# Small matmuls of the head groups in alternating array halves, with two heads' products in two PSUM banks

## The chip, the core and the metric

The kernel runs on one core of a Trainium2 chip. The core has five engines with a queue each: TensorE (PE; its weight loads are shown apart as PEld), VectorE (DVE), ScalarE (ACT), GpSimd (POOL) and SyncE (SP, which here issues most DMAs). Each queue is worked in order, and semaphores tie the queues together. The metric is the device time of one execution in microseconds; lower is better.

## The reference, cut to what matters

The program is one inference step of one decoder layer for a prompt of 512 tokens and 8 single-token samples: modulated RMSNorm, one input projection, two head groups, an output projection and a SwiGLU FFN. The change lies in the two head groups. All data are float32.

The first group is 16 attention heads of 64 columns; for the prompt the three dilated windows fold into one score matrix with a bias per distance:

```
z[q,k]  = (Q_h[q] . K_h[k]) * rn[q] + T_h[q,k]        # q, k = 0..511, causal
out_h   = softmax(z) @ V_h
```

The second group is 16 RWKV-7 heads with a state of 64 x 64 each:

```
S_t = S_{t-1} diag(w_t) + (S_{t-1} a_t) b_t^T + v_t k_t^T ;   y_t = S_t r_t
```

## The kernel before, in words

The 512 tokens of an RWKV head are cut into 8 chunks of 64. Inside a chunk the recurrence is a triangular system, solved with matrix products; between chunks only the state is passed on. Heads are taken in pairs: head 0 of a pair lives in partitions 0 to 63 (`hb[0]`), head 1 in partitions 64 to 127 (`hb[1]`), so most matmuls of this stage use one half of the array's rows, of its columns, or one quarter. There are 8 pairs in each group.

`rwkv_pair(pr)` does for one pair, in this order:

- the Gram products `pg`: per half `i` of the sequence and head `h`, four matmuls of 64 rows x 128 columns, which VectorE masks into `GM` (L901);
- a solve of 16 x 16 blocks: `GM` is written to DRAM (`nd`, L910), read back with one block per partition (`i16`, in the trace `i<-nd`, L915), inverted by nineteen VectorE instructions (`itmp`, `xi`, L926 to L938), written out again (`xd`, L941) and read back as `XX` (four DMAs, L944);
- from the 16 x 16 inverses to the 64 x 64 one by matmuls of quarter array size: `pq` from `XX`, then `px` and `pxt`, then `pq2` and `px2` of 32 x 32 (the trace shows these two as `pq<-X2T,GM` and `px<-X,Q`);
- `pbk`, `pat`, `pgv`, `pu` and last `pxa`, which ScalarE and VectorE empty into `AR` (L1019) and `Mt` (L1020).

`chain(pr)` then passes the state through the 8 chunks (`pch`, with a ScalarE copy into `Sall` after each) and computes the outputs (`zy`, `z2`). `attn_pair(pr)` does one pair of attention heads: scores `pz`, softmax on VectorE and ScalarE, transposes `pzt`, values `po`. Between them stand matmuls of a weight stream for the modulation (`ada`), filler work with no hurry.

Two things set the order. A list puts the pieces in program order (`r0 r1 c0 a0 r2 c1 S a1 r3 c2 a2 ...`: r is `rwkv_pair`, c `chain`, a `attn_pair`, S the RWKV step of the samples), and a scheduler at build time then orders each engine's queue by what it takes to be ready. A tile of a pool can be written only when the tile that last had its buffer has been read; within a pool the buffers go round in program order. The PSUM pools of this stage:

```
NPS, NPA, NPT, NPG, SP, SPL, PER = 1, 2, 2, 1, 1, 8, 4
psa = lambda name: psB.tile([P, 512], F32, tag="psa", name=name, bufs=NPA)
pst = lambda name: psB.tile([P, 512], F32, tag="pst", name=name, bufs=NPT)
pa = lambda name: psB.tile([P, 512], F32, tag="pa", name=name, bufs=NPG)
```

Before the change `pa` (one bank) holds only Gram products. `psa` (two banks) holds everything else in `rwkv_pair`: per pair `pq`, `px`, `pxt`, `pq2`, `px2`, `pbk` twice, `pat`, `pgv`, `pu` twice, `pxa` twice. `pst` (two banks) holds the attention tiles `pz`, `pzt` and `po`. A float32 matmul is two passes through the array, so the trace has two matmul records for each one in the code.

Of the kernel before, what the change touches and what calls it, by code (L numbers as in the profile page):

```python
# [12 lines left out]
ALU = mybir.AluOpType  # L13
# [4 lines left out]
P = 128  # L18
# [60 lines left out]
def hymba_step(tc, a):  # L79
# [97 lines left out]
    with ExitStack() as top:  # L177
# [627 lines left out]
        with ExitStack() as wk_stack:  # L805
# [73 lines left out]
            def rwkv_pair(pr):  # L879
# [88 lines left out]
                for c in range(2):  # L968
                    top_, bot = slice(c * 64, c * 64 + 32), slice(c * 64 + 32, c * 64 + 64)
                    for i in range(8):  # L970
                        mm(pq2[bot, i, :32], gm(i // 2, c, i % 2, top_, slice(c * 64 + 32, c * 64 + 64)), X2T[top_, i, :32])
                Q2 = tq2(f"Q2{pr}", 256).rearrange("p (i t) -> p i t", i=8)
                px2 = psa(f"px2{pr}").rearrange("p (i t) -> p i t", i=8)
                for c in range(2):
                    top_, bot = slice(c * 64, c * 64 + 32), slice(c * 64 + 32, c * 64 + 64)
                    ac.copy(Q2[bot], pq2[bot, :, :32])
                    for i in range(8):
                        mm(px2[top_, i, :32], Q2[bot, i, :], X2[bot, i, 32:])
                    ve.tensor_copy(X2[top_, :, 32:], px2[top_, :, :32])
# [11 lines left out]
                for c in range(2):  # L991
                    for b in range(4):
# [3 lines left out]
                for c in range(2):  # L996
                    for i in range(8):
                        mm(pgv[hb[c], i * 64 : i * 64 + 64], gm(i // 2, c, i % 2, hb[1 - c], hb[c]), UV[hb[1 - c], i // 2 * 2 + c, i % 2, :])
                ac.copy(AG[:, :, 0, :], pgv.rearrange("p (i e) -> p i e", e=E))
                XA = txa(f"XA{pr}", 512).rearrange("p (b h e) -> p b h e", b=4, h=2)  # L1000
                for q in range(2):
                    pu = psa(f"pu{pr}{q}").rearrange("p (b h x e) -> p b h x e", b=2, h=2, x=2)
                    for c in range(2):
                        for i in range(4):
                            mm(pu[hb[c], i // 2, i % 2], X2[hb[c], 4 * q + i, :], AG[hb[c], 4 * q + i])
                    for c in range(2):
                        ac.copy(UV[hb[c], 4 * q + c : 4 * q + 4 : 2], pu[hb[c], :, :, 0, :])
                    ac.copy(XA[:, 2 * q : 2 * q + 2], pu[:, :, :, 1, :])
                Mt = wl.tile([P, 4, 2, E], F32, tag="mt", name=f"Mt{pr}", bufs=NMT)
                for c in range(2):  # L1010
                    pxa = psa(f"pxa{pr}{c}")
                    for i in range(8):
                        o_ = i // 2 * 64
                        mm(pxa[hb[i % 2], o_ : o_ + 64], AG[hb[c], i, 1, :], X2[hb[c], i, :])
                    for i in range(8):
                        b, h = i // 2, i % 2
                        o_ = 256 + b * 64
                        mm(pxa[hb[h], o_ : o_ + 64], XA[hb[c], b, h, :], BKt[hb[c], 2 * b + c, h * 64 : h * 64 + 64])
                    ac.copy(ARv[:, :, 3 * c, :], pxa[:, :256].rearrange("p (b t) -> p b t", b=4))  # L1019
                    ve.tensor_tensor(Mt[:, :, c, :], pxa[:, 256:].rearrange("p (b t) -> p b t", b=4),  # L1020
                                     eye2.unsqueeze(1).to_broadcast([P, 4, E]), op=ALU.add)
                return lambda: chain(pr, AR, Mt, UV, BKt, GM, gm, bv)

            def chain(pr, AR, Mt, UV, BKt, GM, gm, bv):
# [17 lines left out]
                for q in range(2):  # L1042
                    zy = psz(f"zy{pr}{q}").rearrange("p (c e) -> p c e", c=4)
                    for c in range(4):
                        if q or c:
                            mm(zy[:, c, :], AR[:, (4 * q + c) * 128 : (4 * q + c + 1) * 128], S[:, 4 * q + c, :])
                    for c in range(2):
                        n0 = 2 if q == 0 and c == 0 else 0
                        u = UV[hb[c], 4 * q + c + n0 : 4 * q + 4 : 2].rearrange("p b h e -> p b (h e)")
                        ve.tensor_add(u, u, zy[hb[c], c + n0 :: 2, :])  # L1050
                    q2 = slice(2 * q, 2 * q + 2)
                    if q == 0:
                        gp.memset(Y[64:, 0], 0.0)
# [4 lines left out]
                    for c in range(4):  # L1058
                        b, R_ = 2 * q + c // 2, hb[1 - c % 2]
                        for h in range(2):  # L1060
                            mm(z2[R_, c // 2, h * 64 : h * 64 + 64], gm(b, c % 2, h, slice(0, 128), R_), UV[:, 4 * q + c, h, :])
                    ve.tensor_add(Y[:, q2], Y[:, q2], z2[:, :2])
# [99 lines left out]
            def attn_pair(pr):  # L1162
# [14 lines left out]
                def scores(qi):  # L1177
                    nk = 128 * (qi + 1)
                    for h in range(2):
                        hr = slice(h * 64, h * 64 + 64)  # L1180
                        pz = pst(f"pz{pr}{h}{qi}")
                        mm(pz[:, :nk], q[hr, qi * 128 : (qi + 1) * 128], kn[hr, :nk])
                        z = tz(f"z{pr}{h}{qi}", nk)
                        ve.scalar_tensor_tensor(z, in0=pz[:, :nk], scalar=rn[:, qi, h : h + 1], in1=Ts[h][:, 384 - 128 * qi :],  # L1184
# [8 lines left out]
                def values(qi):  # L1193
# [9 lines left out]
                    for h in range(2):  # L1203
# [262 lines left out]
```

## Time and profile before

| what | value |
|---|---|
| median of 3 runs | 3371.26 us (3350.44 to 3377.52) |
| the profiled execution | 3378.55 us; span of its instructions 3376.8 us |
| TensorE busy, share of the span | 88% |
| VectorE busy | 73% |
| ScalarE busy | 38% |
| mean granted TensorE clock | 0.918 of full speed |
| stage of the head groups | from about 895 us to about 1505 us of the span |

The profile is a record of one execution; its times start with the span. "Busy" is the union of the instructions' durations on an engine. A matmul's record ends when its last result leaves the array, while the next one starts much earlier, so a busy TensorE need not be a TensorE at its peak: what a matmul costs in a row of equal ones is the distance from start to start.

### The profile page before, as it was taken

The numbers are of one execution on the slowest core, as the hardware profiler recorded it, in microseconds if no ns is written. First come the engines' busy times: TensorE is split into PE (matmuls) and PEld (weight loads), VectorE is DVE, ScalarE is ACT, GpSimd is POOL, SyncE is SP. The second block draws the span as 40 slices with busy tenths as digits, with TensorE's granted clock in tenths as the row PEclk, the third lists the DMA queues.
The fourth block names the chain that finished last, engine by engine and source line by source line (L and its number), as shares of the span: only waits on it lengthen the run. The fifth ranks groups of instructions, "written<-read, shape, count | busy, mean of one in ns | idle before, by whom it ended". The sixth has DMA issues, their size and how long they took to land.

```text
span 3376.8 us, 59004 instructions
## 1 busy us (share of the span) xinstructions
PE 2981.6 (88%) x23282; PEld 2629.4 (78%) x23282; DVE 2480.9 (73%) x4846; ACT 1278.0 (38%) x2041; POOL 212.9 (6%) x216
## 2 busy tenths in 40 slices
PE   6987888999889999977977999999999987888988
PEld 2477787889746666656967999999999987787878
DVE  5666788777557455656878787778777788889786
ACT  3353343334223343444434333333333343334333
POOL 0100122110012111101000000000000000000000
PEclk8978999999858798887988999999999998999999
DMA  7744444444579798933322333333333332323223
GB/s 255 232 139 154 147 159 157 133 146 140 175 223 282 201 239 232 249 103 117 109 78 69 113 104 104 108 112 107 113 101 113 109 125 96 99 94 119 85 94 104
DMA packets 449194, 476.17 MB, mean 141 GB/s; under 512 B 84110, under 2 KB 360547, under 8 KB 448916
## 3 DMA queue, kind: packets, MB, share of 16 engines
q1 hardware_dynamic: 438736, 452.16, 43.4%
q10 hardware_dynamic: 7428, 11.65, 1.0%
q0 software_dynamic: 2752, 8.60, 0.8%
q8 instruction: 182, 2.98, 0.4%
q14 instruction: 96, 0.79, 0.1%
HBM read 409.10 MB, written 68.17 MB: 141 GB/s over the span
## 4 chain that ended last, share of the span: by engine, by line
PE 35%; DVE 28%; DMA 23%; issue 5%; ACT 5%; SPq 1%; POOL 1%; ACTq 0%; DVEq 0%; POOLq 0%
PE ada L90 4%; DMA raw_ada<-in_ada_w 2%; SPq L130 1%; PE po L90 1%; DVE x_a L125 1%; PE lx L90 1%; PE pg L90 1%; PE pz L90 1%; PE px L90 1%; DMA K<-in_cache_k 1%; PE pch L90 1%; PE pq L90 1%; DMA xb<-in_ada_w 1%; PE q22M L90 1%; PE q31M L90 1%
## 5 line engine op out<-in xcount | busy, mean ns | idle before, releaser
L90 PE MATMUL ada<-raw_ada,c_st 128*32 128x512 f32 x584 | 123.7, 763 | 17.5 <-DMA raw_ada<-in_ada_w 16.8
L90 PE MATMUL ada<-xb,c_st 128*32 128x512 f32 x184 | 69.9, 673 | 15.9 <-DMA xb<-in_ada_w 13.8
L1037 ACT ACTIVATE Sall<-pch,ppl 64x64 f32<-64x64 f32 x128 | 39.5, 309 | 75.5 <-PE pch L90 57.7
L1238 POOL TENSOR_TENSOR K<-K,qb 128x1024 f32<-128x1024 f32 (+2 forms) x24 | 58.2, 2440 | 147.5 <-DMA K<-in_cache_k 91.6
L1188 ACT ACTIVATE z<-z,mx 128x128 f32<-128x128 f32 (+3 forms) x64 | 35.8, 560 | 78.2 <-DVE mx L1187 37.9
L90 PEld LDWEIGHTS pg<-AR,BK 64*128 64x128 f32 x256 | 41.0, 237 | 22.7 <-issue 11.9
L90 PE MATMUL pz<-ak,aq 64*128 64x256 f32 (+3 forms) x128 | 55.3, 581 | 0.7 <-DMA ak<-pqd 0.7
L90 PE MATMUL pg<-AR,BK 64*128 64x128 f32 x256 | 49.1, 342 | 6.1 <-DMA AR<-abd 2.7
L90 PE MATMUL g0M<-x_g,g0hl 128*128 128x260 f32 x168 | 31.3, 348 | 21.7 <-ACT x_g L124 7.4
L90 PE MATMUL po<-zt,av 128*64 128x128 f32 x320 | 49.1, 310 | 0.4 <-ACT zt L1200 0.4
L90 PE MATMUL o0M<-x_m,o0hl 128*128 128x260 f32 x168 | 33.5, 366 | 17.6 <-ACT x_m L124 14.2
L901 DVE TENSOR_TENSOR GM<-pg,cst 128x512 f32<-128x512 f32 x32 | 22.0, 688 | 36.5 <-PE pg L90 36.3
L198 PEld LDWEIGHTS pzt<-ident,z 128*128 128x128 f32 x160 | 19.0, 155 | 37.5 <-ACT z L1190 13.0
L1184 DVE SCALAR_TENSOR_TENSOR z<-pz,rnq,T 128x128 f32<-128x128 f32 (+3 forms) x64 | 34.4, 546 | 18.3 <-PE pz L90 16.2
L90 PEld LDWEIGHTS g0M<-x_g,g0hl 128*128 128x128 f32 x168 | 27.5, 241 | 25.4 <-ACT x_g L124 8.7
L90 PEld LDWEIGHTS o0M<-x_m,o0hl 128*128 128x128 f32 x168 | 29.7, 259 | 21.6 <-ACT x_m L124 17.5
L1412 DVE SCALAR_TENSOR_TENSOR y<-c_d,modT,y 128x512 f32<-128x512 f32 x64 | 45.9, 751 | 0.0
L90 PEld LDWEIGHTS ada<-raw_ada,c_st 128*32 128x32 f32 x584 | 16.4, 119 | 37.4 <-DMA raw_ada<-in_ada_w 22.7
L1200 ACT COPY zt<-pzt 128x128 f32<-128x128 f32 (+3 forms) x64 | 26.5, 426 | 49.5 <-PE pzt L198 41.1
L90 PEld LDWEIGHTS po<-zt,av 128*64 128x64 f32 x320 | 34.2, 151 | 13.3 <-issue 6.8
L198 PE MATMUL pzt<-ident,z 128*128 128x128 f32 x160 | 33.8, 321 | 11.8 <-ACT z L1190 10.0
L1190 ACT ACTIVATE z<-z,mx 128x128 f32<-128x128 f32 (+3 forms) x64 | 35.5, 559 | 16.8 <-DVE mx L1189 11.6
(2104 smaller groups left out, 9215.3 us busy)
## 6 DMA issues: line engine op xcount, KB each, us to landing
raw_ada<-in_ada_w SPq DMA_DIRECT2D x64, 1024.0 KB
xb<-in_ada_w SPq DMA_DIRECT2D x92, 256.0 KB
actd<-c_u SPq DMA_DIRECT2D x22, 520.0 KB
a<-actd SPq DMA_DIRECT2D x22, 520.0 KB
raw_ada<-in_ada_w SPq DMA_DIRECT2D x36, 256.0 KB
lsd<-lx SPq DMA_DIRECT2D x12, 520.0 KB
prd<-rkv SPq DMA_DIRECT2D x24, 256.0 KB
K<-in_cache_k SPq DMA_DIRECT2D x16, 384.0 KB
```

The costliest lines, as they stand in the source:

```text
L90: pe.matmul(out, lhsT=lhsT, rhs=rhs, start=start, stop=stop)
L125: ve.tensor_sub(x[:, 1, o:e], src, x[:, 0, o:e].bitcast(F32))
L130: sp.dma_start(raw.rearrange("p (k m) c -> p k (m c)", k=2), src[k * P : (k + 2) * P, :].rearrange("(k p) m -> p k m", p=P))
L198: pe.transpose(out, in_=in_, identity=ident[:n, 0:n])
L901: ve.tensor_tensor(GM[i][:, :, :, h], pg, gmask.unsqueeze(2).to_broadcast([P, 2, 2, P]), op=ALU.mult)
L1037: ac.activation(S[hb[h], ch + 1, hb[h]], pc_[hb[h], ch, :], AF.Copy, scale=ppl[hb[h], pr, ch : ch + 1])
L1184: ve.scalar_tensor_tensor(z, in0=pz[:, :nk], scalar=rn[:, qi, h : h + 1], in1=Ts[h][:, 384 - 128 * qi :], op0=ALU.mult, op1=ALU.add)
L1188: ac.activation(z, z, AF.Exp, bias=mx[:, 0:1], accum_out=mx[:, 1:2])
L1190: ac.activation(z, z, AF.Copy, scale=mx[:, 2:3])
L1200: ac.copy(zt, pzt[:, :nk])
L1238: OK.tensor_mul(K[:n], K[:n], qb[:n])
L1412: ve.scalar_tensor_tensor(y[:, f, :SEQ], in0=c[:, j, :SEQ], scalar=modT[:, 48 + f, 0:1], in1=y[:, f, :SEQ], op0=ALU.mult, op1=ALU.add)
```

## The change

In nine places the loops around small matmuls are turned inside out, so that consecutive matmuls in program order use different halves of the array's rows, of its columns, or of both. In three places this needs two tiles at once: the Gram products of the two heads (head 0 stays in `pa`, head 1 goes to the pool `psa`), the two tiles of `pxa`, and the scores of the two heads. The number of matmuls, their sizes and their inputs stay the same, and so do the copies that follow. The diff, cut to its core:

```diff
                 for i in range(2):
+                    pg = [f(f"pg{pr}{i}{h}").rearrange("p (b c t) -> p c b t", b=2, c=2) for h, f in enumerate((pa, psa))]
+                    for b in range(2):
+                        for c in range(2):
+                            cc = slice((4 * i + 2 * b + c) * 128, (4 * i + 2 * b + c + 1) * 128)
+                            for h in range(2):
+                                mm(pg[h][:, c, b, :], BK[hb[h], cc], AR[hb[h], cc])
                     for h in range(2):
-                        rows = slice(h * 64, h * 64 + 64)
-                        pg = pa(f"pg{pr}{i}{h}").rearrange("p (b c t) -> p c b t", b=2, c=2)
-                        for b in range(2):
-                            for c in range(2):
-                                cc = slice((4 * i + 2 * b + c) * 128, (4 * i + 2 * b + c + 1) * 128)
-                                mm(pg[:, c, b, :], BK[rows, cc], AR[rows, cc])
-                        ve.tensor_tensor(GM[i][:, :, :, h], pg, gmask.unsqueeze(2).to_broadcast([P, 2, 2, P]), op=ALU.mult)
+                        ve.tensor_tensor(GM[i][:, :, :, h], pg[h], gmask.unsqueeze(2).to_broadcast([P, 2, 2, P]), op=ALU.mult)
...
-                for c in range(2):
-                    for i in range(8):
+                for i in range(8):
+                    for c in range(2):
                         mm(pq[hb[c], i, :], E1f[hb[c], i, :], XX[1][hb[c], i, :])
...
-                for c in range(2):
-                    for i in range(8):
+                for i in range(8):
+                    for c in range(2):
                         mm(px[hb[c], i, :], Q[hb[c], i, :], XX[0][hb[c], i, :])
+                for i in range(8):
+                    for c in range(2):
                         mm(pxt[hb[c], i, :], XX[0][hb[c], i, :], Q[hb[c], i, :])
...
+                pxa = [psa(f"pxa{pr}{c}") for c in range(2)]
+                for i in range(8):
+                    o_ = i // 2 * 64
+                    for c in range(2):
+                        mm(pxa[c][hb[i % 2], o_ : o_ + 64], AG[hb[c], i, 1, :], X2[hb[c], i, :])
...
                     nk = 128 * (qi + 1)
+                    pzs = [pst(f"pz{pr}{h}{qi}") for h in range(2)]
                     for h in range(2):
-                        hr = slice(h * 64, h * 64 + 64)
-                        pz = pst(f"pz{pr}{h}{qi}")
-                        mm(pz[:, :nk], q[hr, qi * 128 : (qi + 1) * 128], kn[hr, :nk])
+                        mm(pzs[h][:, :nk], q[hb[h], qi * 128 : (qi + 1) * 128], kn[hb[h], :nk])
+                    for h in range(2):
                         z = tz(f"z{pr}{h}{qi}", nk)
...
-                    for h in range(2):
-                        hr = slice(h * 64, h * 64 + 64)
-                        for j in range(qi + 1):
-                            mm(po[hr, :128], vt_[:, j, hr], zts[qi, h][:, j * 128 : (j + 1) * 128], start=(j == 0), stop=(j == qi))
+                    for j in range(qi + 1):
+                        for h in range(2):
+                            mm(po[hb[h], :128], vt_[:, j, hb[h]], zts[qi, h][:, j * 128 : (j + 1) * 128], start=(j == 0), stop=(j == qi))
```

Left out of it: the same turn of the loops for `pq2`, `px2`, `pat`, `pgv`, `pu` and `z2`, and for the second half of `pxa`.

Since the scheduler makes the final order, it has to be read from the built programs. Three places follow. In a tile's name the first digit is the pair and the last number the buffer's serial number: `pg201` is the Gram product of pair 2, half 0, head 1.

TensorE before, around the Gram products of pair 2 (half 1, heads 0 and 1) and the first product `pq1` of pair 1:

```order
L90 MATMUL pg210_10164<-AR2_10141,BK2_10142 128x128 x4
L90 MATMUL pz113_10747<-ak1_10646,aq1_10645 128x512
L198 MATMUL pzt102_10756<-ident_63,z102_10706 128x128 x3
L90 MATMUL pq1_9535<-XX11_9523,E11_9530 64x64 x8
L90 MATMUL pch0_9737<-Sall0_9132,Mt0_9420 64x64 x2
L90 MATMUL pq1_9535<-XX11_9523,E11_9530 64x64 x8
L90 MATMUL ada11_10096<-raw_ada11_0_10097,c_st_82 32x512 x4
L90 MATMUL ada11_10096<-raw_ada11_4_10103,c_st_82 32x512 x4
L90 MATMUL pg211_10170<-AR2_10141,BK2_10142 128x128 x4
```

TensorE after the change, around the Gram products of head 1 of the same pair 2:

```order
L90 MATMUL pxa10_9699<-BKt1_9631,XA1_9673 64x64
L90 MATMUL pxa11_9700<-BKt1_9631,XA1_9673 64x64
L90 MATMUL pov1_10839<-V10_10840,pts_10831 32x256 x4
L90 MATMUL pov1_10839<-V11_10846,pts_10831 32x256 x4
L90 MATMUL pov1_10839<-V12_10852,pts_10831 32x256 x4
L90 MATMUL ada14_10918<-raw_ada14_0_10919,c_st_82 32x512 x4
L90 MATMUL ada14_10918<-raw_ada14_4_10925,c_st_82 32x512
L90 MATMUL pg201_10153<-AR2_10141,BK2_10142 128x128
L90 MATMUL pch1_10419<-Sall1_9133,Mt1_9698 64x64 x2
L90 MATMUL pg201_10153<-AR2_10141,BK2_10142 128x128 x3
L90 MATMUL pg211_10165<-AR2_10141,BK2_10142 128x128 x4
```

The last Gram products of pair 2 stood beside the first quarter-size product of pair 1; now they stand behind the last product `pxa` of pair 1. The products of head 0 (`pg200`, `pg210`) stay far ahead of them, four in a row, so the two heads' products do not alternate.

TensorE, from before to the change, at the values and scores of attention pair 0:

```order
-L90 MATMUL po_9910<-zt_9903,av_9825 64x128 x2
+L90 MATMUL po_9910<-zt_9903,av_9825 64x128
 L90 MATMUL ada_9136<-sel_67,adac_9161 128x9 x4
-L90 MATMUL po_9910<-zt_9908,av_9825 64x128 x2
+L90 MATMUL po_9910<-zt_9908,av_9825 64x128
+L90 MATMUL po_9910<-zt_9903,av_9825 64x128
+L90 MATMUL po_9910<-zt_9908,av_9825 64x128
 L90 MATMUL pz_9916<-ak_9824,aq_9823 128x512
-L90 MATMUL pz_9925<-ak_9824,aq_9823 128x512
+L90 MATMUL pz_9917<-ak_9824,aq_9823 128x512
```

The values of the two heads now take turns; the two scores stood next to each other here already.

VectorE after the change, from the last product of pair 2 to the inversion of pair 3:

```order
L1025 TENSOR_TENSOR Mt2_10380<-pxa20_10381,eye2_9130 128x4x64
L1025 TENSOR_TENSOR Mt2_10380<-pxa21_10382,eye2_9130 128x4x64
L1211 COPY at3_12089<-po32_12206 128x128
L901 TENSOR_TENSOR GM30_10972<-pg301_10975,cst_9118 128x4x128
L901 TENSOR_TENSOR GM31_10973<-pg311_10987,cst_9118 128x4x128
L248 TENSOR_TENSOR modT_69<-ada17_11637,adab_72 128x36
L1376 SCALAR_TENSOR_TENSOR A1_76<-modT_69,n2g_71 128x36
L1211 COPY at3_12089<-po33_12228 128x128
L926 TENSOR_TENSOR itmp3_11006<-i163_11002,xi3_11004 64x2
L928 TENSOR_REDUCE xi3_11004<-itmp3_11006 64x2
```

Before, VectorE's part of this inversion (`itmp3`) stood 51 rows ahead of `Mt2`; now it stands 8 rows behind, with three instructions between it and the masking of pair 3's Gram products.

## Rows read from the trace of the kernel before

**Rows 1.** Windows: us, busy per engine, granted clock, DMA share, GB/s.

```profile
1350.00:1400.00 50.00, 49.34 (x545) 33.96 (x544) 28.10 (x83) 22.87 (x64) 7.65 (x7) 0.97 0.91 256
...
1500.00:1550.00 50.00, 24.59 (x143) 17.69 (x142) 30.44 (x71) 16.59 (x35) 4.41 (x6) 0.61 0.29 98
...
895.00:1505.00 610.00, 553.59 (x5248) 375.00 (x5245) 339.19 (x826) 227.58 (x612) 95.77 (x76) 0.80 0.81 226
```

**Rows 2.** Tiles on TensorE, whole span: first and last start in us.

```profile
L90 PE MATMUL pq<-XX,E x256: 218/267/366, 975.8 to 1442.5; 64*64 64x64 f32 x128
L90 PE MATMUL pxa<-BKt,XA x256: 218/218/366, 1026.3 to 1480.9; 64*64 64x64 f32 x128
```

**Rows 3.** The same within pair 2 and pair 7.

```profile
L90 PE MATMUL pq<-XX,E x32: 311/311/366, 1100.0 to 1103.0; 64*64 64x64 f32 x32
L90 PE MATMUL pxa<-BKt,XA x32: 218/218/218, 1143.5 to 1145.2; 64*64 64x64 f32 x32
L90 PE MATMUL pq<-XX,E x32: 218/218/267, 1440.8 to 1442.5; 64*64 64x64 f32 x32
```

**Rows 4.** TensorE in order of time: start, length, merged equal instructions.

```profile
1207.99 0.93 PE L90 MATMUL pg<-AR,BK 64*128 64x128 f32 x6 [0.44 <-DMA BK<-abd]
1208.85 0.68 PE L90 MATMUL pxa<-X,AG 64*64 64x64 f32 x16
1209.37 0.46 PE L90 MATMUL pxa<-BKt,XA 64*64 64x64 f32 x10
...
1372.76 1.85 PE L90 MATMUL pq<-XX,E 64*64 64x64 f32 x32
1374.54 1.09 PE L90 MATMUL po<-zt,av 128*64 128x128 f32 x8
```

**Rows 5.** The same: scores of one head, and of two heads next to each other.

```profile
980.62 1.22 PE L90 MATMUL pz<-ak,aq 64*128 64x256 f32 x2
981.77 0.47 PE L90 MATMUL px<-XX,Q 64*64 64x64 f32 x2
...
1116.09 1.23 PE L90 MATMUL pz<-ak,aq 64*128 64x256 f32 x4
1117.25 0.26 PE L198 MATMUL pzts<-ident,zs 16*96 16x16 f32 x1
```

**Rows 6.** Group of the values on TensorE by form: count, busy us, mean ns.

```profile
L90 PE MATMUL po<-zt,av 128*64 128x128 f32 x320 | 49.1, 310 | 0.4 <-ACT zt L1200 0.4
```

**Rows 7.** VectorE, masking of the Gram products of pair 2 and pair 6.

```profile
L901 DVE TENSOR_TENSOR GM<-pg,cst x4: 681/690/692, 1018.6 to 1040.7; 128x512 f32<-128x512 f32 x4
L901 DVE TENSOR_TENSOR GM<-pg,cst x4: 692/692/692, 1293.4 to 1321.2; 128x512 f32<-128x512 f32 x4
```

**Rows 8.** SyncE's queue, pair 6: when the DMAs of the solve were issued.

```profile
1321.92 1.25 SPq L910 DMA_DIRECT2D nd<-GM  x2
...
1325.47 0.60 SPq L915 DMA_DIRECT2D i<-nd  x1
...
1349.29 0.84 SPq L941 DMA_DIRECT2D xd<-xi  x1
...
1356.86 1.28 SPq L944 DMA_DIRECT2D XX<-xd  x2
...
1361.81 4.60 SPq L944 DMA_DIRECT2D XX<-xd  x2
```

**Rows 9.** VectorE, the same pair: first and last instruction of the inversion.

```profile
1330.08 0.15 DVE L926 TENSOR_TENSOR itmp<-i,xi 64x2 f32<-64x2 f32 x1
...
1347.93 0.36 DVE L938 COPY xi<-xi 64x256 f32<-64x256 f32 x1
```

**Rows 10.** VectorE, the long instructions of all eight inversions: min, median, max ns.

```profile
L931 DVE TENSOR_TENSOR itmp<-i,xi x8: 994/1004/2544, 930.1 to 1400.0; 64x512 f32<-64x512 f32 x8
L935 DVE TENSOR_TENSOR itmp<-xi x8: 1066/1082/1121, 931.9 to 1404.5; 64x512 f32<-64x512 f32 x8
```

**Rows 11.** ScalarE, the copy that empties `pxa` of pair 7.

```profile
1481.23 0.35 ACT L1019 COPY AR<-pxa 128x256 f32<-128x256 f32 x1
```

More of the change, by code (lines that the diff above doesn't have):

```diff
@@ L967, in rwkv_pair @@
                 pq2 = psa(f"pq2{pr}").rearrange("p (i t) -> p i t", i=8)
[L968 to L971, printed above, removed]
+                ht_ = [(slice(c * 64, c * 64 + 32), slice(c * 64 + 32, c * 64 + 64)) for c in range(2)]
+                for i in range(8):
+                    for c, (top_, bot) in enumerate(ht_):
+                        mm(pq2[bot, i, :32], gm(i // 2, c, i % 2, top_, bot), X2T[top_, i, :32])
                 Q2 = tq2(f"Q2{pr}", 256).rearrange("p (i t) -> p i t", i=8)
                 px2 = psa(f"px2{pr}").rearrange("p (i t) -> p i t", i=8)
-                for c in range(2):
-                    top_, bot = slice(c * 64, c * 64 + 32), slice(c * 64 + 32, c * 64 + 64)
+                for top_, bot in ht_:
                     ac.copy(Q2[bot], pq2[bot, :, :32])
-                    for i in range(8):
+                for i in range(8):
+                    for top_, bot in ht_:
                         mm(px2[top_, i, :32], Q2[bot, i, :], X2[bot, i, 32:])
+                for top_, bot in ht_:
                     ve.tensor_copy(X2[top_, :, 32:], px2[top_, :, :32])
@@ L990, in rwkv_pair @@
                 pat = psa(f"pat{pr}")
-                for c in range(2):
-                    for b in range(4):
+                for b in range(4):
+                    for c in range(2):
                         mm(pat[hb[c], b * 128 : (b + 1) * 128], ARv[:, b, 3 * c, :], ident)
@@ L995, in rwkv_pair @@
                 pgv = psa(f"pgv{pr}")
-                for c in range(2):
-                    for i in range(8):
+                for i in range(8):
+                    for c in range(2):
                         mm(pgv[hb[c], i * 64 : i * 64 + 64], gm(i // 2, c, i % 2, hb[1 - c], hb[c]), UV[hb[1 - c], i // 2 * 2 + c, i % 2, :])
@@ L1002, in rwkv_pair @@
                     pu = psa(f"pu{pr}{q}").rearrange("p (b h x e) -> p b h x e", b=2, h=2, x=2)
-                    for c in range(2):
-                        for i in range(4):
+                    for i in range(4):
+                        for c in range(2):
                             mm(pu[hb[c], i // 2, i % 2], X2[hb[c], 4 * q + i, :], AG[hb[c], 4 * q + i])
@@ L1009, in rwkv_pair @@
                 Mt = wl.tile([P, 4, 2, E], F32, tag="mt", name=f"Mt{pr}", bufs=NMT)
-                for c in range(2):
[L1011 to L1020, printed above, removed]
+                pxa = [psa(f"pxa{pr}{c}") for c in range(2)]
+                for i in range(8):
+                    o_ = i // 2 * 64
+                    for c in range(2):
+                        mm(pxa[c][hb[i % 2], o_ : o_ + 64], AG[hb[c], i, 1, :], X2[hb[c], i, :])
+                for i in range(8):
+                    b, h = i // 2, i % 2
+                    o_ = 256 + b * 64
+                    for c in range(2):
+                        mm(pxa[c][hb[h], o_ : o_ + 64], XA[hb[c], b, h, :], BKt[hb[c], 2 * b + c, h * 64 : h * 64 + 64])
+                for c in range(2):
+                    ac.copy(ARv[:, :, 3 * c, :], pxa[c][:, :256].rearrange("p (b t) -> p b t", b=4))
+                    ve.tensor_tensor(Mt[:, :, c, :], pxa[c][:, 256:].rearrange("p (b t) -> p b t", b=4),
                                      eye2.unsqueeze(1).to_broadcast([P, 4, E]), op=ALU.add)
@@ L1057, in chain @@
                     z2 = psz(f"z2{pr}{q}").rearrange("p (b e) -> p b e", b=4)
-                    for c in range(4):
+                    for n in range(8):
+                        c, h = n // 4 * 2 + n % 2, n // 2 % 2
                         b, R_ = 2 * q + c // 2, hb[1 - c % 2]
-                        for h in range(2):
-                            mm(z2[R_, c // 2, h * 64 : h * 64 + 64], gm(b, c % 2, h, slice(0, 128), R_), UV[:, 4 * q + c, h, :])
+                        mm(z2[R_, c // 2, h * 64 : h * 64 + 64], gm(b, c % 2, h, slice(0, 128), R_), UV[:, 4 * q + c, h, :])
                     ve.tensor_add(Y[:, q2], Y[:, q2], z2[:, :2])
@@ L1202, in values @@
                     po = pst(f"po{pr}{qi}")
-                    for h in range(2):
-                        hr = slice(h * 64, h * 64 + 64)
-                        for j in range(qi + 1):
-                            mm(po[hr, :128], vt_[:, j, hr], zts[qi, h][:, j * 128 : (j + 1) * 128], start=(j == 0), stop=(j == qi))
+                    for j in range(qi + 1):
+                        for h in range(2):
+                            mm(po[hb[h], :128], vt_[:, j, hb[h]], zts[qi, h][:, j * 128 : (j + 1) * 128], start=(j == 0), stop=(j == qi))
                     ve.tensor_copy(at[:, qi * 128 : (qi + 1) * 128], po[:, :128])
```

2 lines of the change are left out of this document (1 added, 1 removed).

## The prediction, made before the run

> **What bounds the kernel now.** I read the windows first, to see which engine fills the stage that the change touches; then when the first and the last product of each pair start, for the stage's rhythm; then single stretches of TensorE, for what one pass costs with and without alternation; last the queues between a pair's Gram products and its first quarter-size product, since the order of the built program moves exactly that stretch.
>
> From 895 to 1505 us TensorE is busy 553.59 of 610 us, VectorE 339.19, ScalarE 227.58, and the DMA engines hold a share of 0.81 [rows 1]. So TensorE bounds this stage today. Eight pairs go through it: the first `pq` starts at 975.8, that of pair 7 at 1440.8, which is 465.0 / 7 = 66.4 us per pair [rows 2, 3]. The reader should note that this rhythm is not the latency of a pair. From `pq` to the start of the last `pxa` a pair takes 1145.2 - 1100.0 = 45.2 us (pair 2) or 1480.9 - 1440.8 = 40.1 (pair 7) [rows 2, 3]; from the start of its last masking to its `pq` it takes 1100.0 - 1040.7 = 59.3 (pair 2) or 1372.8 - 1321.2 = 51.6 (pair 6) [rows 3, 4, 7]. Together about 100 us, in a rhythm of 66: the solve of one pair runs while the pair before is in its matrix products. That overlap is possible because the Gram products have a PSUM bank of their own.
>
> **Part one: passes that alternate.** Sixteen passes of `pxa`, which already changed column halves from matmul to matmul, take 1209.37 - 1208.85 = 0.52 us, 33 ns each. Thirty-two passes of `pq`, of the same 64 x 64 size but eight matmuls in one quarter and then eight in the other, take 1374.54 - 1372.76 = 1.78 us, 56 ns each [rows 4]. So alternation is worth 23 ns a pass. `pq`, `px`, `pxt` and `pgv` have 32 passes per pair each, 128 in all: 128 x 23 ns = 2.9 us per pair, 23.6 us for eight. `pu`, `pat`, `pq2` and `px2`, 144 passes per pair of other sizes, lie between nothing and the same 23 ns (26 us); I take 10 us. `pxa`, which now changes row halves too, could at most halve its 33 ns (64 passes, 1 us per pair), and `z2` changed halves at every second matmul already: I take nothing for both. Eight passes of `po`, one head's in a row, last 1.09 us to the end of the last; with 0.31 us for that one alone a pass costs (1.09 - 0.31) / 7 = 111 ns [rows 4, 6]. In the new order 112 of 160 follow one of the other head, where 12 did: 200 passes at half the price, 200 x 56 ns = 11 us. Sum: 23.6 + 10 + 11, about 45 us less TensorE time.
>
> **What doesn't happen.** The Gram and score products were to alternate as well. They could: two heads' scores of 256 columns next to each other take 1117.25 - 1116.09 = 1.16 us, and one head's alone 981.77 - 980.62 = 1.15 [rows 5]. But in the built program 10 of 128 Gram products follow one of the other half, where 3 did, and 15 of 64 scores, where 13 did. I book nothing for them.
>
> **Part two: the Gram products wait for other banks.** Head 1's Gram tiles now come from `psa`. Its two banks go round in program order, and the tiles ahead of pair n+1's are the two `pxa` of pair n. So `pg` of head 1 can't start before pair n's last product has been copied out, and behind it stands the whole solve of pair n+1: masking, `nd`, `i16`, inversion, `xd`, `XX`, `pq`. The order shows it: `pg201` and `pg211` right behind pair 1's `pxa`, the inversion on VectorE eight rows behind `Mt` where it stood 51 rows ahead. What overlapped is now one chain, and its length per pair is A + H + B:
>
> A, `pq` to the last `pxa`: 45.2 and 40.1 before; less about 4 us for the passes above; and fewer other products stand in between (of pair 7, 176 matmuls instead of 258, 160 of them its own). I take 38 us for the pairs that still have filler beside them, and 28 (40.1 x 176 / 258 = 27.4) for the late ones: the last product of the weight stream stands inside pair 4 now, inside pair 7 before.
>
> H, from there to the last masking: the copy 0.35 us [rows 11], sixteen passes of `pg` at 0.86 / 6 = 0.14 us (1207.99 to 1208.85 [rows 4]), 2.3 us, one masking 0.69 [rows 7]: 3.4; with a row or two of other work 4.5 us.
>
> B, the solve: 59.3 and 51.6 before. Its legs in pair 6 [rows 7 to 9]: masking to `i<-nd` 1325.5 - 1321.2 = 4.3, to the first inversion instruction 4.6, inversion to its last instruction 1347.9 - 1330.1 = 17.9, to the last `xd` 1.4, to `XX` 7.6, its four DMAs 4.9, to `pq` 11.0. Only the inversion was stretched by other work on VectorE; alone, its two longest instructions take 1.0 and 1.1 us [rows 10] and the other seventeen, at 0.15 to 0.36 like the first and the last [rows 9], 2.6 to 6.1: some 6.5 us, and B 40. The lower bound is thus 40, the upper 59. VectorE and SyncE will have less beside it than before but still other rows: I take 48 us for the early and 45 for the late pairs, nearer to pair 6, the one with the least beside it. Both queues are in order: behind an inversion that waits for `i16` stand the sums of `chain` into `UV` and `Y` and the softmax of the next scores, and behind a `pq` that waits for `XX` stand the next `pz`, `pzt` and the weight stream, so other engines can't use the gap in full.
>
> A + H + B is 90.5 us early and 77.5 late. Of the seven steps from pair to pair I count four early and three late: 4 x 90.5 + 3 x 77.5 = 594.5 us instead of 465.0, +129.5. The last pair's own A is 28 instead of 40.1, -12. The tail behind it stays. The 45 us of TensorE time are not taken off again: as far as they lie on the chain they are in A, the rest is time in which TensorE now waits. Against the profiled execution that is 3378.55 + 117 = 3496 us; it stands 7 us above the median of the runs shown, so I say **3490 us**.
>
> On the point of PSUM the Trainium skill speaks against this change: "TensorEngine Tiling (Array Packing)", section "Restrictions and Gotchas", says that row tiling raises PSUM pressure, because different row tiles write to different banks. The trace agrees as far as it shows the two heads' scores side by side in two banks at the price of one [rows 5]; what the second bank costs elsewhere no row of before shows. By the page alone the sum would not change, only its sign becomes less surprising.
>
> **The rivals.** *Faster, the packing wins.* If TensorE stays the bound, the 45 us come off: 3371 - 45 = 3326 us. For it speaks the 553.59 of 610 us. It decides if A + H + B stays within 66.4 us, that is B under 66.4 - 38 - 4.5 = 24 us early or 34 late; the shortest B above is 51.6, the bound 40. A chance of 0.10, mostly for a reading of the order that is wrong.
>
> For this rival the Trainium skill gives more: "TensorE: Matmul & The Clock Gate", Part 3 on packing small matmuls, has a pack of tiles take one matmul's time plus about 4 ns for each further tile. By it a quarter pass would go from 56 to 28 + 2 ns instead of 33, and the rival to about 3320. The trace shows the halving for scores [rows 5] and nearly so for `pxa` [rows 4].
>
> *No change.* With emptier queues the solve shrinks to its bound and the late pairs' A with it, 27 + 3.6 + 40 = 71 us for all seven steps: 495, +30, less 13, 3388 us; that is within 1%. Chance 0.08.
>
> *Slower yet, the clock.* TensorE waits in the longer steps, and the stage shows that a less busy TensorE is granted less: 0.61 where it is busy 24.59 of 50 us, 0.97 where 49.34 [rows 1]. Between its two levels, 1.2 and 2.4 GHz, the mean over the stage is 0.80. At 0.61 the matrix products in A take up to 0.80 / 0.61 = 1.31 times as long, 12 us more per step, 7 x 12 = 84: about 3575 us. Chance 0.20.
>
> **How the numbers follow.** Forecast 0.62 (3400 to 3540), clock 0.20, no change 0.08, faster 0.10. All bounds low give 3388, all high (45 + 5 + 59 = 109 us a step, 763 instead of 465) 3674. Leaving out no more than 2 in 10 the range is 3395 to 3640. Within 1% (about what a measurement of this kernel can tell from no change) means 3338 to 3405: slower 0.82, same 0.08, faster 0.10.
>
> **What would show it.** In the profile of the changed kernel: `pq` to `pq` some 78 to 92 us instead of 66; `pg` of a pair in two clusters, the second just behind the `pxa` of the pair before; GM to `pq` at 40 to 55 us with TensorE idle ahead of `pq`, `XX` or the inversion named as what ended the wait; `pq` at about 33 ns a pass; scores and Gram products no cheaper; TensorE's share of the stage well under 0.9, least in the late pairs. The prediction is wrong if `pq` follows `pq` in 66 us or less, or if the time is lost outside 895 to 1505 us, since the order there is the same.

## Result and the profile after

The changed kernel takes 3471.59 us (median of 4, 3453.27 to 3474.89) against 3374.08 for the kernel before (3350.44 to 3377.52): a ratio of 1.029, 95% interval 1.023 to 1.035. The forecast was 3490 us, slower. The profiled execution took 3471.38 us, 92.8 more than the one before.

First the windows of the changed kernel, for the stretch of [rows 1], for the whole stage, which is now 100 us longer, and for the time ahead of it.

```profile
895.00:1505.00 610.00, 461.36 (x4540) 285.64 (x4541) 294.06 (x740) 191.70 (x520) 78.46 (x67) 0.74 0.74 216
895.00:1605.00 710.00, 534.02 (x5253) 337.66 (x5252) 335.75 (x843) 227.03 (x615) 89.33 (x76) 0.72 0.67 195
0.00:870.00 870.00, 750.21 (x5186) 645.72 (x5187) 626.71 (x1330) 341.52 (x531) 101.52 (x122) 0.94 0.51 166
```

TensorE does the stage's 5250 matmul records in 534 us instead of 554, so alternation saves engine time; but it was idle for 56 us of 610 and is idle for 176 of 710. Nothing was lost elsewhere: ahead of the stage it is busy 750 us (757.64 before), and from the last `z2` to the end of the span the two traces differ by 2 us (1871 and 1873). The last `z2` (in the trace `z<-UV,GM`; here before and after, with first and last start) ends at 1598.5 instead of 1504.1, 94.4 us later, which is the whole loss.

```profile
L90 PE MATMUL z<-UV,GM x128: 219/222/369, 1332.3 to 1503.8; 128*64 128x64 f32 x128
...
L90 PE MATMUL z<-UV,GM x160: 221/314/370, 1334.1 to 1598.2; 128*64 128x64 f32 x160
```

The tile view of `pq` gives the rhythm, to be set beside [rows 2]:

```profile
L90 PE MATMUL pq<-XX,E x256: 217/311/367, 972.9 to 1556.1; 64*64 64x64 f32 x128
```

Its first starts per pair are 972.9, 1073.4, 1171.6, 1261.6, 1359.9, 1416.8, 1483.3 and 1551.8. The seven steps sum to 578.9 us, 82.7 each, where they were 66.4. Split into the prediction's three parts, from the same view of `pq`, `pxa` and `GM` (A: `pq` to the end of the last `pxa`; H: to the start of the next pair's last masking; B: to its `pq`), in us:

| step | A | H | B | sum |
|---|---|---|---|---|
| 0 to 1 | 29.1 | 9.2 | 62.2 | 100.5 |
| 1 to 2 | 35.4 | 15.1 | 47.7 | 98.2 |
| 2 to 3 | 50.8 | 4.6 | 34.6 | 90.0 |
| 3 to 4 | 44.7 | 5.9 | 47.7 | 98.3 |
| 4 to 5 | 31.7 | 3.5 | 21.7 | 56.9 |
| 5 to 6 | 25.6 | 11.0 | 29.9 | 66.5 |
| 6 to 7 | 26.6 | 7.1 | 34.8 | 68.5 |
| pair 7 | 25.0 | | | |

TensorE in order of time between pair 4's `pu` and pair 5's solve shows the new chain itself:

```profile
1388.39 1.16 PE L90 MATMUL pg<-AR,BK 64*128 64x128 f32 x8
...
1391.02 0.57 PE L90 MATMUL pxa<-BKt,XA 64*64 64x64 f32 x22
...
1392.76 0.94 PE L90 MATMUL pg<-AR,BK 64*128 64x128 f32 x7
1393.63 0.33 PE L90 MATMUL pch<-Sall,Mt 64*64 64x64 f32 x4
1393.89 1.16 PE L90 MATMUL pg<-AR,BK 64*128 64x128 f32 x8
```

The `pg` of 1388 is a head-0 tile, made ahead for pair 6. The head-1 tiles of pair 5, at 1392.76 and 1393.89, come 1 to 2 us behind pair 4's last `pxa`. Then VectorE and SyncE's queue, for the solve of the same pair:

```profile
1395.09 0.69 DVE L901 TENSOR_TENSOR GM<-pg,cst 128x512 f32<-128x512 f32 x1 [0.66 <-PE pg L90]
1401.89 0.15 DVE L926 TENSOR_TENSOR itmp<-i,xi 64x2 f32<-64x2 f32 x1 [6.11 <-DMA i<-nd]
...
1409.95 0.36 DVE L938 COPY xi<-xi 64x256 f32<-64x256 f32 x1
```

```profile
1399.46 0.59 SPq L915 DMA_DIRECT2D i<-nd  x1
1409.72 1.29 SPq L941 DMA_DIRECT2D xd<-xi  x2
1412.22 2.63 SPq L944 DMA_DIRECT2D XX<-xd  x4
```

VectorE has nothing to do for 6.1 us until `i` lands. Before, this solve ran beside the products of the pair ahead of it: pair 6's last masking came at 1321.2 [rows 7], while the last `pxa` of pair 5 came 34 us later:

```profile
1354.85 0.63 PE L90 MATMUL pxa<-BKt,XA 64*64 64x64 f32 x16
```

### The profile page after: what moved, and what is told of

It is laid out like the page before. It is cut to its first block, busy times and chain, and to the rows that moved or that the text cites. A ratio compares the mean times of both kernels' runs of the same rounds, so it can differ in the third digit from the quotient of the medians.

```text
span 3469.6 us, 59018 instructions
## 1 busy us (share of the span) xinstructions
PE 2955.5 (85%) x23282; PEld 2583.4 (74%) x23282; DVE 2470.8 (71%) x4846; ACT 1275.3 (37%) x2041; POOL 204.8 (6%) x216
## 4 chain that ended last, share of the span: by engine, by line
DVE 23%; PE 20%; DMA 18%; ACT 4%; issue 3%; SPq 1%; POOL 0%; ACTq 0%; DVEq 0%; POOLq 0%
DMA raw_ada<-in_ada_w 1%; PE ada L90 1%; DMA K<-in_cache_k 1%; SPq L130 1%; DVE x_a L125 1%; DMA a<-actd 1%; DMA BK<-abd 1%; PE pch L90 1%; PE po L90 1%; DMA XX<-xd 1%; PE pg L90 1%; PE g9M L90 1%; PE g19M L90 1%; PE g8M L90 0%; PE g2M L90 0%
## 5 line engine op out<-in xcount | busy, mean ns | idle before, releaser
L90 PE MATMUL ada<-xb,c_st 128*32 128x512 f32 x184 | 68.9, 673 | 17.3 <-DMA xb<-in_ada_w 15.5
L90 PE MATMUL pz<-ak,aq 64*128 64x128 f32 (+3 forms) x128 | 55.4, 601 | 10.7 <-DVE at L1211 7.9
L1243 DVE TENSOR_REDUCE lg<-K 128x16 f32<-128x1024 f32 (+2 forms) x24 | 29.2, 1216 | 49.5 <-POOL K L1242 49.3
L1242 POOL TENSOR_TENSOR K<-K,qb 128x1024 f32<-128x1024 f32 (+2 forms) x24 | 56.0, 2345 | 125.7 <-DMA K<-in_cache_k 100.5
L198 PEld LDWEIGHTS pzt<-ident,z 128*128 128x128 f32 x160 | 21.9, 172 | 51.6 <-ACT z L1195 19.3
L90 PE MATMUL g0M<-x_g,g0hl 128*128 128x260 f32 x168 | 31.3, 348 | 21.7 <-ACT x_g L124 7.5
L90 PE MATMUL po<-zt,av 128*64 128x128 f32 x320 | 42.3, 338 | 2.8 <-ACT zt L1205 2.1
L1205 ACT COPY zt<-pzt 128x128 f32<-128x128 f32 (+3 forms) x64 | 26.6, 425 | 48.9 <-PE pzt L198 48.4
L90 PEld LDWEIGHTS o0M<-x_m,o0hl 128*128 128x128 f32 x168 | 28.7, 252 | 21.3 <-ACT x_m L124 16.2
L901 DVE TENSOR_TENSOR GM<-pg,cst 128x512 f32<-128x512 f32 x32 | 21.8, 687 | 31.8 <-PE pg L90 31.7
```

The source lines that it names most:

```text
L90: pe.matmul(out, lhsT=lhsT, rhs=rhs, start=start, stop=stop)
L198: pe.transpose(out, in_=in_, identity=ident[:n, 0:n])
L1205: ac.copy(zt, pzt[:, :nk])
L1242: OK.tensor_mul(K[:n], K[:n], qb[:n])
L1243: ve.tensor_reduce(lg[:n, i, :], K[:n].rearrange("p (g e) -> p g e", e=E), axis=AX.X, op=ALU.add)
```

## Experiments

Times are medians; ratios, with their 95% intervals, are to the kernel before on the same chip.

**1. Gram products back in one bank** (the rest of the change kept).

```diff
-pg = [f(f"pg{pr}{i}{h}")... for h, f in enumerate((pa, psa))]   # heads in turns
+pg = pa(f"pg{pr}{i}{h}")...                                     # one head, then the other
```

> The changed kernel with its Gram products put back as they were: both heads one after the other through the one bank of pa; all other alternation stays. Theory (banks): the whole loss comes from head 1's Gram tiles in psa, which put the solve of a pair behind the last product of the pair before. Without that the rhythm returns to 66 us per pair or less, TensorE is the bound again, and its saving of about 45 us shows: 3310 to 3350 us. Rival (array): alternating halves itself costs, by drains, by a lower granted clock or by the new order of the queues; then most of the loss stays, 3430 to 3480 us.

3327.66 us, 0.987 (0.980 to 0.994). In its trace the stage is back in its old overlap, at 55.6 us a step:

```profile
L90 PE MATMUL pq<-XX,E x256: 217/218/367, 972.8 to 1369.4; 64*64 64x64 f32 x128
```

The Gram part of the change costs 144 us of 3471.59 (medians from two chips), and the rest gains 50. In the profiled executions the last `z2` ends 73.9 us earlier than before (1430.2), and the span is 56.6 us shorter: the work behind the stage, the same instructions, took 1890 us instead of 1873. Over all the versions it takes from 1871 to 1896 us with no relation to the edit that I can see, so differences of under 25 us between the whole times of two single executions are not read here. Run again on another chip:

> The version with the Gram products put back into their single bank, once more, on the chip that runs the other kernels of this set. Theory (all alternation outside the Gram products is worth about 45 us): 3320 to 3340 us, a ratio of 0.982 to 0.992 to the kernel before. Rival (the first measurement was favoured by its chip): a ratio of 0.993 to 1.000.

3322.92 us, 0.984 (0.977 to 0.991): it holds.

**2. The Gram part alone** (everything else as before).

> The kernel before with nothing changed but the Gram products of the two heads, written in turns into pa and psa. Theory (banks): the steps from pair to pair grow as in the changed kernel, about 97 us early and 64 late, and no saving is set against it: 3470 to 3520 us. Rival (array): the Gram products hardly alternate in the built order, so nothing much moves: 3360 to 3390 us.

3514.06 us, 1.042 (1.035 to 1.049).

**3. The bank alone**: the old loops and order, head 1's tile from the other pool.

```diff
-pg = pa(f"pg{pr}{i}{h}")...
+pg = (pa, psa)[h](f"pg{pr}{i}{h}")...
```

> The kernel before in its own loop order, one head's four Gram products after the other's; only the tile of head 1 is taken from psa instead of pa. No product alternates that did not before. Theory (banks): the pool alone makes the wait, so the time is that of the run with the Gram products in turns, within 1%: 3460 to 3520 us. Rival (array): without turns nothing is lost: 3360 to 3390 us.

3516.37 us, 1.043 (1.036 to 1.050), the same as with the turns; 83.9 us a step. So the turns of the Gram products cost and give nothing that these runs can tell (each ratio is known to 0.7%); the bank is all of it. TensorE in order of time shows `pg` behind the last `pxa` of pair 3 here too; pair 4's `nd` is issued from 1292.2 us on:

```profile
1287.77 0.68 PE L90 MATMUL pxa<-BKt,XA 64*64 64x64 f32 x15
1288.38 1.06 PE L90 MATMUL ada<-raw_ada,c_st 128*32 128x512 f32 x8
1289.38 0.71 PE L90 MATMUL pg<-AR,BK 64*128 64x128 f32 x4
```

**4. Both banks kept, another program order**: loads, Gram products and masks of pair n+1 are written ahead of pair n's solve.

```diff
+for n in range(pr, min(pr + 2, NPR)):
+    if n not in grams:
+        grams[n] = gram(n)
```

> The changed kernel, head 1's Gram tiles still in psa, but the loads and Gram products of pair n+1 are written ahead of the solve of pair n, so that their turn in psa comes before pair n's pq and not after its pxa. Theory (banks): it is the place in the round of psa that costs and not the pool; the solve of a pair overlaps again with the products of the pair before, and the time is 3310 to 3370 us. Rival (array, or a pool too small by itself): two banks for five more tiles per two pairs are too few wherever they stand, or alternation costs: 3430 us or more.

3336.82 us, 0.989 (0.983 to 0.995), 58.0 us a step. With its tiles taken from the pool before pair n's own, head 1 no longer waits for pair n's `pxa`. So not the use of two banks costs, but the place in the pool's rotation. (Loads and masks moved ahead together with the tiles, and what they give by themselves this run doesn't separate; in experiment 3 it is the tile's place alone that costs.)

**5. Parts of the alternation.** Quarter products and `z2` alone (Gram, scores and values as before):

> The changed kernel with Gram products, scores and values put back: only the products inside the solve and behind it (pq, px, pxt, pq2, px2, pat, pgv, pu, pxa) and z2 alternate. By the prediction's sum these are 23.6 + 10 = 34 us of the 45 us of TensorE time: 3335 to 3350 us. Rival (latency): these products stand on the chain of a pair, whose other legs overlap anyway, so most of it is hidden: 3365 to 3380 us.

3356.8 us, 0.9947 (0.9918 to 0.9977): 18 us by the ratio, half of the 34 expected, and between the two ranges. The values alone, on the kernel before:

> The kernel before with only the values po of the two heads in turns. By the prediction's sum 11 us less TensorE time: 3360 to 3370 us. Rival: taking turns makes the first value wait for the second head's transposes, which costs as much as it saves: 3375 to 3385 us.

3388.81 us, 1.0044 (1.0013 to 1.0075): a miss, above both ranges; by the ratio they lose 15 us alone. The scores' pairing alone:

> The kernel before with only the scores pz of the two heads written into two tiles taken at once. In its built order 13 of 64 scores follow one of the other half, as before, so the prediction has nothing for it: 3365 to 3385 us. Rival: holding both banks of pst for the two scores delays the transposes and values that share them: 3390 us or more.

3371.06 us, 0.9998 (0.9967 to 1.0028): nothing. Quarters and values together, without scores and Gram:

> The changed kernel with the Gram products and the scores put back, so that the quarter products, z2 and the values po alternate. Quarters alone gave 3356.8 us, with values and scores as well 3327.7 us, while values alone on the kernel before gave 3388.8 us. Theory (the values' turns are worth 10 to 15 us in themselves, and the loss of values alone came from another order of the work): 3325 to 3345 us. Rival (the 29 us between those two kernels are an effect of the order that the scores' pairing brings, and the values' turns are worth nothing): 3350 to 3375 us.

3326.56 us, 0.986 (0.980 to 0.992), as fast as version 1. So the two parts are worth about 50 us together, and not the sum of what each does alone (18 less and 15 more). Each variant is also ordered anew; what of the difference is that order stays open.

**6. What makes the early steps longer than the late ones** (96.8 against 64.0 us). First the stream's pieces were moved late in the list that sets the program order:

```diff
-"f2 r0 r1 c0 a0 f3 r2 c1 S a1 f3 r3 c2 a2 f3 r4 c3 a3 f3 r5 c4 a4 f3 r6 ..."
+"r0 r1 c0 a0 r2 c1 S a1 r3 c2 a2 r4 c3 a3 r5 c4 a4 f8 r6 c5 a5 f8 r7 ..."
```

> The changed kernel with the weight stream of the stage written behind the fifth attention pair and later instead of beside every pair; nothing else differs. The late steps of the changed kernel were shorter than forecast, and the early ones not. Theory (stream): the weight stream's transfers lengthen the DMA legs of the solve wherever they run, so the first four steps from pq to pq shrink from about 97 us towards 75 and the last three grow from about 64 towards 85; the total moves little, 3440 to 3490 us. Rival (samples): the early steps are long because of the sample steps and of the cache reads beside the first pairs; then the early steps stay above 90 us.

3452.6 us, 1.023 (1.019 to 1.026), but it doesn't answer the question: the stream's loads were issued from 925 to 1340 us, much as in the changed kernel (913 to 1356), so nothing had moved late. Its early steps take 94.7 us and its late ones 68.6. The first `pq` starts 33 us earlier (940.3) than in the changed kernel, and the last `z2` ends 29 us earlier (1569.8); that start is what it gained. Then the stream's bytes were cut, with the number of its loads and matmuls kept:

```diff
-AQ.dma_start(raw, src...)            # four blocks of weights
+AQ.dma_start(raw[:, :1], src[:P]...) # the first of the four, used four times
```

> The changed kernel, with a quarter of the bytes of the modulation weight stream inside the head-group stage: every load of four weight blocks fetches only the first of the four, and the four matmul groups use that one block (three quarters of that part of the modulation weights are left out; the number of loads, of matmuls and the order are kept). In the changed kernel the steps from one pair's pq to the next take 96.8 us for the first four and 64.0 us for the last three. Theory (the early steps are longer because the solve's DRAM round trip and the loads share the DMA engines with the stream, which is over before the late pairs): the early steps fall to 65 to 80 us, and the execution to 3370 to 3420 us. Rival (the early steps are longer because of the other work on TensorE and VectorE, the 8 samples' products and the cache reads, and not because of the stream's bytes): the early steps stay above 90 us, and the time above 3450 us.

3413.71 us (one execution). The early steps fall to 83.3 us on average and the late ones stay at 64.3: between the two expectations. With the cut go 13.5 of the 32.8 us between early and late steps: 6.7 in A (40.0 to 33.3) and 7.8 in B (48.1 to 40.3), with H 1.1 longer. But the bytes are not the only thing that changed. The expectation says that the order is kept, and that is not so: the scheduler put the stream's matmuls further ahead in TensorE's queue. The four early steps hold 200, 120, 112 and 32 of their records, where the changed kernel has 120, 112, 104 and 128, and the step with 32 still takes 79.0 us. So the 13.5 us belong to the bytes and the new place together.

From the first `xd` to `pq` the early pairs take 11.5 us on average instead of 15.5, the late ones of the changed kernel 7.5. What makes up the remaining 19.3 us is shown for pair 1 alone. Its B is 62.2 us in the changed kernel and 60.1 with the cut, and VectorE's lines between the inversion's first instruction and `xd` show why, in the changed kernel (1026 to 1055 us):

```profile
L1144 DVE TENSOR_TENSOR tm<-S,T 128x1024 f32<-128x1024 f32 x2 | 2.4, 1221 | 0.0
L1136 DVE TENSOR_TENSOR tm<-S,dv 128x1024 f32<-128x1024 f32 x2 | 2.4, 1210 | 0.0
L926 DVE TENSOR_TENSOR itmp<-i,xi 64x2 f32<-64x2 f32 (+6 forms) x7 | 2.4, 346 | 0.1
```

The state step of the 8 single-token samples, 1.2 us an instruction, stands between those of the inversion: fifteen of them, some 18 us, in an inversion that takes 30.0 us here and 8.4 in pair 5. For pairs 2 to 4 no run separates the causes.

The same cut in the kernel before:

> The kernel before with the same cut of the weight stream to a quarter of its bytes (three quarters of that part of the modulation weights are left out). In the kernel before the solve of a pair lies beside the chain work of the pair before it, so its length should matter less. Theory (overlap hides the DMA legs): the steps stay within 5 us of 66.4, and the execution within 40 us of 3374. Rival (the stream's bytes also bound the kernel before, by the loads or by TensorE's matmuls waiting for them): the steps fall below 58 us, and the time below 3320 us. The difference between this run and the one above is then what the bank placement costs without the stream's bytes; by the theory it is 30 to 80 us instead of 98 to 140.

3381.97 us (one execution), steps of 61.8 us, within the 5 us of the theory. The whole time shows no gain, but the stage does: its last product (here a `po`, at 1484.4) ends 20 us earlier than before, and the work behind it, which the edit doesn't touch, took 1896 us instead of 1873. TensorE is busy 559 of 610 us from 895 to 1505:

```profile
895.00:1505.00 610.00, 559.42 (x5341) 379.74 (x5340) 346.61 (x868) 232.49 (x626) 98.37 (x79) 0.84 0.55 146
```

With the cut in both, the change as a whole costs 31.7 us in the whole time, and 40.8 by the end of the stage (1525.2 against 1484.4). Both lie in the 30 to 80 us that were expected; two single executions tell no more.

## Why the prediction was right, and where its terms were off

**The step that decided.** Part two said that head 1's Gram tiles stand behind pair n's `pxa` and that the solve thereby joins the chain. Versions 1 to 4 show it: the bank alone gives +138 us, taking it back or taking the tile earlier removes it all. The first rival, that alternation wins because TensorE stays the bound, named its point: a step within 66.4 us. The late steps meet it on average (64.0), the early ones by far don't.

**The sum.** Seven steps were to take 594.5 us and took 578.9; the last A was to be 28 and is 25.0. From there: the first `pq` 2.9 us earlier, steps +113.9, last A -15.3, what follows it -1.3, together +94.4, where +117 was forecast. Behind this lie errors of both signs:

- A: 38 and 28 forecast, 40.0 and 28.0 measured (means of four early and three late steps). Right.
- H: 4.5 forecast, 8.7 and 7.2 measured, 25 us too little over the stage. The copy, `pg` and the mask are priced rightly, but in an ordered queue other work stands between them.
- B, early: 48 forecast, 48.1 measured, with single steps from 34.6 to 62.2. That the mean agrees is luck in part: pair 1's 62.2 hold the state step of the samples, which the prediction didn't price.
- B, late: 45 forecast, 28.8 measured, 49 us too much, and below the bound of 40 that I had called the lowest. In pair 5 (the rows above) masking to `i` takes 4.4 us (4.3 in the prediction), the inversion up to its first `xd` 7.8 (6.5 + 1.4 to the last), both as priced. But `i` to the inversion takes 2.4 instead of 4.6, `xd` to `XX` 2.5 instead of 7.6, and `XX` to `pq` 4.6 instead of 15.9. I had taken only the inversion for stretched by other work, and carried the other legs of pair 6 over. They were stretched too. In SyncE's queue of the kernel before, `gg` stood for 5.0 us between pair 6's `xd` and its first `XX`, and a load of the stream and two of the cache stood between the first two `XX` and the last two:

```profile
1351.29 5.00 SPq L1088 DMA_DIRECT2D gg<-lsd  x1
...
1358.19 1.05 SPq L236 DMA_DIRECT2D raw_ada<-in_ada_w  x1
1359.34 2.42 SPq L1227 DMA_DIRECT2D V<-in_cache_v  x2
```

In pair 5 of the changed kernel nothing stands between `xd` and the last `XX`. The stream's loads were also running beside pair 6, and I had worked out myself that the stream ends inside pair 4. In pair 2 of the changed kernel, with the stream and with `gg` in the way, `xd` to `XX` is 5.2 us, and `XX` to `pq` 11.5:

```profile
1154.96 1.30 SPq L941 DMA_DIRECT2D xd<-xi  x2
1156.32 2.75 SPq L1093 DMA_DIRECT2D gg<-lsd  x1
1159.16 0.39 SPq L236 DMA_DIRECT2D raw_ada<-in_ada_w  x1
1160.14 2.63 SPq L944 DMA_DIRECT2D XX<-xd  x4
```

How much of it is the stream is shown in part only: in experiment 6 `xd` to `pq` of the early pairs fell from 15.5 us to 11.5 and not to the 7.5 of the late ones.

**The alternation's 45 us.** Version 1 gained 50, version 5's pair of parts 52. By group, busy us on TensorE in the stage, before:

```profile
L90 PE MATMUL px<-XX,Q 64*64 64x64 f32 x256 | 40.5, 267 | 0.1
L90 PE MATMUL pxt<-Q,XX 64*64 64x64 f32 x256 | 39.9, 264 | 0.0
L90 PE MATMUL pq<-XX,E 64*64 64x64 f32 x256 | 22.0, 265 | 0.0
...
L90 PE MATMUL pgv<-UV,GM 64*64 64x64 f32 x256 | 15.5, 221 | 0.0
...
L90 PE MATMUL px<-X,Q 32*32 32x32 f32 x256 | 12.9, 199 | 0.0
```

and in the changed kernel:

```profile
L90 PE MATMUL po<-zt,av 128*64 128x128 f32 x320 | 42.3, 338 | 2.8 <-ACT zt L1205 2.1
...
L90 PE MATMUL pq<-XX,E 64*64 64x64 f32 x256 | 16.9, 291 | 6.1 <-DMA XX<-xd 6.0
...
L90 PE MATMUL px<-XX,Q 64*64 64x64 f32 x256 | 15.0, 303 | 2.9 <-ACT Q L956 2.9
L90 PE MATMUL pxt<-Q,XX 64*64 64x64 f32 x256 | 12.9, 278 | 0.0
...
L90 PE MATMUL pxa<-BKt,XA 64*64 64x64 f32 x256 | 9.7, 239 | 0.0
L90 PE MATMUL pxa<-X,AG 64*64 64x64 f32 x256 | 9.5, 235 | 2.1 <-ACT XA L1011 1.9
L90 PE MATMUL pgv<-UV,GM 64*64 64x64 f32 x256 | 9.2, 221 | 0.3 <-ACT BKt L990 0.3
L90 PE MATMUL px<-X,Q 32*32 32x32 f32 x256 | 6.5, 198 | 1.4 <-ACT Q L977 1.1
```

`pq` fell from 22.0 to 16.9 and `pgv` from 15.5 to 9.2 (23 ns a pass would be 5.9 each: right). The largest saving is in `px` and `pxt`. Before, their matmuls took turns with each other inside one quarter, so the two lines count much of the same time; together they occupied TensorE for 43.8 us, and now for 26.3, which is 17.5 less where 23 ns a pass give 11.8. The values fell from 49.1 [rows 6] to 42.3, not by 11. `pxa`, for which I took nothing, fell from 21.2 to 16.2 (both lines together, shared time counted once), and `pu`, `pat`, `pq2` and `px2` (here `px<-X,Q`) by 13.0 where I took 10; `z2` grew by 1.9. In all it is 52 us where 45 were booked, near by errors of both signs, and at a granted clock of 0.72 instead of 0.80.

With the bank in place the clock is the same on both sides. Experiment 3, in its stage, to be set beside 534.02 us of the changed kernel:

```profile
895.00:1615.00 720.00, 601.23 (x5254) 401.96 (x5252) 332.04 (x828) 226.71 (x612) 89.60 (x76) 0.72 0.67 192
```

TensorE is busy 67 us less, but the execution gains 45, 3516.37 to 3471.59; of this the profiled executions show 15.6 by the end of the stage (8.2 in the steps, 6.3 in the last A), and the remainder behind it, where they scatter by as much. That most of it would turn into waiting was thus right for the steps; where the rest of the 45 lies stays open.

**What was to be seen.** `pq` to `pq` 78 to 92 us: 82.7 on average, though of the seven steps only the one of 90.0 lies there. GM to `pq` 40 to 55 us: 47.7 in two of seven. Two clusters of `pg`: yes. Gram products and scores no cheaper: experiments 2 and 3 and the scores' pairing alone say so. TensorE's share of the stage 0.75, well under 0.9, but not least in the late pairs (302.54 of 385 us from 975 to 1360, 151.12 of 190 from there to 1550). And the idle time was not ahead of `pq`, which waits 6.1 us for `XX` in all. In an ordered queue it falls to whatever stands first:

```profile
PE ada L90 <- DMA raw_ada<-in_ada_w: 43.6, 16, 6.0
PE pzt L198 <- ACT z L1195: 16.5, 2, 15.6
PE z L90 <- ACT Y L1061: 15.3, 10, 2.9
PE pg L90 <- DMA BK<-abd: 10.7, 3, 6.7
```

(waits of TensorE from 895 to 1605: total us, times, longest).

**The clock rival** was not needed. The granted clock fell from 0.80 to 0.72 in the stage, but late A came out at the 28 us that no clock term had lengthened. What the lower clock cost the rest of the stage no run separates. It shows in single passes. TensorE in order of time, and the windows of the same two stretches:

```profile
972.95 1.15 PE L90 MATMUL pq<-XX,E 64*64 64x64 f32 x32
974.03 1.09 PE L198 MATMUL pzt<-ident,z 128*128 128x128 f32 x8
...
1361.28 1.97 PE L90 MATMUL pq<-XX,E 64*64 64x64 f32 x30
1363.17 0.34 PE L198 MATMUL pzts<-ident,zs 16*97 16x16 f32 x1
```

```profile
972.90:974.00 1.10, 1.10 (x36) 1.01 (x32) 0.00 (x0) 0.00 (x0) 0.00 (x0) 1.00 1.18 197
1361.20:1363.10 1.90, 1.90 (x31) 1.78 (x30) 0.33 (x2) 1.65 (x6) 0.00 (x0) 0.50 0.79 298
```

At the full 2.4 GHz a `pq` pass takes 1.08 / 32 = 34 ns, the 33 that was forecast; at 1.2 GHz 1.89 / 30 = 63 ns, more than the 56 ns that it took without alternation at the full clock [rows 4]. These are averages over a row with its longer gaps at both ends. Inside the rows the trace's single records start 6 and 52 ns apart at the full clock, 58 for two passes or 29 each, where one quarter alone took 58 for each pass; at 1.2 GHz two passes take 107. The prediction's estimate by the Trainium skill ("TensorE: Matmul & The Clock Gate", Part 3: one matmul's time plus about 4 ns for each further tile) was 30 ns a pass. Inside the row the trace agrees, with 29; over the whole row it shows 34.

## What to carry to other kernels

Before a tile moves to another PSUM pool, count which tile stands ahead of it in that pool's rotation and when that one is emptied: here a free second bank was worth nothing in speed, and its place in the rotation cost 4.2 to 4.3%, which taking the tile earlier in program order gave back. When a change turns overlapped stages into a chain, measure each leg where the queues and the traffic are as empty as they will be then, not where it happens to lie today. Alternating small products by themselves is worth having, version 1 being 1.3 to 1.6% faster than the kernel before, but the built order decides how much alternates.

## What the runs showed of the hardware

Products that go round all four quarters, rows and columns both, are cheaper again than those that alternate halves: from 32 passes of `pxa` at 1305.68 to what follows at 1306.26 it is 18 ns each, where sixteen that changed only column halves took 33 ns each [rows 4]. The granted clock was 1.00 in both stretches. In the single records four passes start 7, 7, 6 and 39 ns apart, 59 ns for the four, as much as two passes take in alternating halves and one pass of `pq` in one quarter.

```profile
1305.68 0.65 PE L90 MATMUL pxa<-BKt,XA 64*64 64x64 f32 x32
1306.26 1.92 PE L90 MATMUL ada<-raw_ada,c_st 128*32 128x512 f32 x14
```

A busy TensorE is not always granted more. From 1500 to 1550 us it is busy 44.53 of 50 us at a granted clock of 0.59; in [rows 1] 49.34 of 50 had 0.97, and 24.59 had 0.61.

```profile
1500.00:1550.00 50.00, 44.53 (x338) 28.60 (x337) 26.14 (x65) 21.88 (x65) 10.86 (x9) 0.59 0.34 84
```
